# A three-branch hybrid layer: decays carried in place in the third branch's scan, and another split of the attention's products

## The chip, the cores and the metric

The kernel runs on one core of a Trainium2 chip, as one launch. The number reported is the device time of one execution in microseconds; the figure for the kernel before is the median of three such runs, 2732.86 us (2730.51 to 2734.73). A separate execution was taken by the hardware profiler; it took 2729.9 us, and its span, from the first instruction to the last, is 2728.1 us.

The core's engines work side by side, each through its own instructions in order: TensorE (PE, with its weight loads shown as PEld), VectorE (DVE), ScalarE (ACT), GpSimd (POOL), and SyncE (SP), which here issues the DMAs. They meet only at semaphores.

## The reference, cut to what matters

Sixteen meta tokens go ahead of 2048 tokens of width 1024. After a normalization, one wide projection feeds three mixers of four heads each (head size 128): stick-breaking attention, a gated delta rule, and HGRN2. Their outputs are gated, projected back and summed. The change lies in the first and the third.

The attention's weight of a key is its own sigmoid times the product of the "not taken" sigmoids of all later keys:

```python
log_keep = jnp.where(mask, jax.nn.log_sigmoid(-z), 0.0)
log_passed = lax.cumsum(log_keep, axis=3, reverse=True) - log_keep
attn = jnp.where(mask, jnp.exp(jax.nn.log_sigmoid(z) + log_passed), 0.0)
```

The third branch is a linear recurrence whose state decays per channel; inside a chunk every pair of tokens i >= j needs the product of the decays between them:

```python
a = jnp.einsum('bhid,bhjd,bhijd->bhij', q_c, k_c, dec)
o = o_inter + jnp.einsum('bhij,bhje->bhie', a, v_c)
state = state * jnp.exp(g_end)[:, :, 0, :, None] + jnp.einsum('bhcd,bhce->bhde', k_c * jnp.exp(g_end - g_c), v_c)
```

## The kernel before, in words

**Quarters and dense work.** The 2048 tokens are worked in four quarters of 512 (j = 0 to 3). A generator, `dense_work`, makes all projections of a quarter, the branch products and the output projection: groups of 8 x 3 matmuls of 512 columns. Every fp32 value is split into a rounded high part and a low remainder, and a product is three passes, high by high, high by low, low by high (`mm3`, L176 to L178). A second set of generators makes the sequential parts: `sb_scan` (attention, one head at a time), `gdn_mats` and `gdn_scan` (second branch), `hg_scan` (third branch, two heads at a time, so two passes a quarter and eight in all). `weave` interleaves a scan with dense work by planned microseconds: a scan's `yield 5.0` lets about so much dense work be written between two of its steps. The tile framework then orders the instructions of each engine by its own timeline model, so what stands in the program may move a little.

**The attention's scan.** For each block of keys and each of four 128-query tiles i, `weights` makes the scores z on TensorE, two sigmoids on ScalarE (L533, L534), copies the carry of the block before into the end of `pc` (L538, GpSimd), a running product over the keys on VectorE (L539), and multiplies the sigmoid by it (L545, `at`). That product is on VectorE for tiles 0 and 2 and on GpSimd for tiles 1 and 3. `values` then transposes the four tiles (L567), rounds the high part on ScalarE (L578) and forms the low part on VectorE (L127), and adds to the output `av` by three passes: `mm3` with lh, ll the values' high and low part and ath, atl the weights' high and low part. The order of passes is lh by ath, lh by atl, ll by ath.

**The third branch's scan.** `hg_scan` finds the within-chunk matrix by seven levels, s = 1, 2, 4 ... 64. At level s the chunk is cut into pairs of blocks of s tokens; the rows of the right block against the columns of the left one are a plain product, once each query carries the decays from its block's start and each key those to its block's end. The kernel before keeps two running decay tiles per head, `pf` (from the block's start, in place of the forget gate) and `sf` (to the block's end). At each level, for each head, VectorE writes a fresh tile `kql`: right halves q x pf (L1151), left halves k x sf (L1155; at s = 1 a copy on GpSimd, L1153). TensorE multiplies it with itself in small tiles into `z` (L1160), VectorE or ScalarE picks the wanted parts (L1208, L1195, L1202), and VectorE brings `sf` and `pf` to the next block size (L1223, L1224; at s = 1 a copy and a fill on GpSimd, L1220, L1221). After the last level q x pf and k x sf are formed over 512 tokens (L1231, L1233), the latter is transposed to tokens, and a scan over four sub-blocks of 128 updates the state (L1244 to L1249). Each kql is a tile of its own in a pool of 21 buffers (tag S), so VectorE may make the next levels' while TensorE has not reached them.

## Time and profile before

| | |
|---|---|
| median of three runs | 2732.86 us |
| profiled execution | 2729.9 us, span 2728.1 us |
| PE busy | 2690.0 us, 99% of the span |
| PEld, DVE, ACT, POOL busy | 2243.4, 1432.5, 961.0, 717.7 us |
| granted TensorE clock, mean | 0.999 |

In the rows of groups, "acc<-xh,w ... x2096 | 796.8, 380" gives how many records there are, their busy time in us, and the mean of one in ns; what stands after the next bar is the engine's idle time ahead of them and what ended it. Matmuls overlap in the pipeline, so their durations add to more than the time that passes. A matmul of fp32 operands that is no transpose has two records. The table by windows gives, for stretches of the span, the busy time of each engine.

### The profile page before, as it was taken

The numbers are of one execution on the slowest core, as the hardware profiler recorded it, in microseconds if no ns is written. First come the engines' busy times: TensorE is split into PE (matmuls) and PEld (weight loads), VectorE is DVE, ScalarE is ACT, GpSimd is POOL, SyncE is SP. The second block draws the span as 40 slices with busy tenths as digits, with TensorE's granted clock in tenths as the row PEclk, the third lists the DMA queues.
The fourth block names the chain that finished last, engine by engine and source line by source line (L and its number), as shares of the span: only waits on it lengthen the run. The fifth ranks groups of instructions, "written<-read, shape, count | busy, mean of one in ns | idle before, by whom it ended". The sixth has DMA issues, their size and how long they took to land.

```text
span 2728.1 us, 46691 instructions
## 1 busy us (share of the span) xinstructions
PE 2690.0 (99%) x17984; PEld 2243.4 (82%) x17984; DVE 1432.5 (53%) x2870; ACT 961.0 (35%) x2199; POOL 717.7 (26%) x989
## 2 busy tenths in 40 slices
PE   7999999999999999999999999999999999999999
PEld 6998888888888888888888888888888887787887
DVE  5476647645357734443255765554325568556422
ACT  5564343343346212212144641321214456313120
POOL 4555213433133401112122332111212223302111
PEclk9999999999999999999999999999999999999999
DMA  7667756679554654557755456355774454554556
GB/s 263 221 234 251 256 178 221 231 268 320 195 180 146 205 177 130 157 158 241 231 190 171 156 168 205 106 158 155 248 221 140 163 168 143 164 161 122 160 163 213
DMA packets 200834, 521.08 MB, mean 191 GB/s; under 512 B 42848, under 2 KB 44832, under 8 KB 200612
## 3 DMA queue, kind: packets, MB, share of 16 engines
q1 hardware_dynamic: 200324, 518.03, 59.0%
q8 instruction: 142, 2.33, 0.3%
q14 instruction: 80, 0.66, 0.1%
q10 hardware_dynamic: 288, 0.07, 0.0%
HBM read 397.57 MB, written 120.44 MB: 190 GB/s over the span
## 4 chain that ended last, share of the span: by engine, by line
PE 92%; DVE 5%; DMA 1%; ACT 1%; issue 1%; POOL 0%; SPq 0%; DVEq 0%; ACTq 0%; POOLq 0%
PE acc L176 20%; PE acc L177 20%; PE acc L178 20%; PE av L176 5%; PE av L177 5%; PE av L178 5%; PE tr L567 2%; PE t L389 2%; PE z L1160 1%; PE z L176 1%; PE z L177 1%; PE z L178 1%; PE z L864 1%; PE tr L389 1%; PE tr L1245 1%
## 5 line engine op out<-in xcount | busy, mean ns | idle before, releaser
L176 PE MATMUL acc<-xh,w 128*128 128x512 f32 (+2 forms) x2096 | 796.8, 380 | 5.6 <-DVE y L1293 1.7
L177 PE MATMUL acc<-xl,w 128*128 128x512 f32 (+2 forms) x2096 | 790.0, 377 | 0.3 <-DVE xl L269 0.2
L178 PE MATMUL acc<-xh,w 128*128 128x512 f32 (+2 forms) x2096 | 786.7, 375 | 0.0
L176 PEld LDWEIGHTS acc<-xh,w 128*128 128x128 f32 x2096 | 396.1, 189 | 75.2 <-DVE y L1293 2.2
L178 PEld LDWEIGHTS acc<-xh,w 128*128 128x128 f32 x2096 | 396.4, 189 | 66.2 <-issue 0.2
L177 PEld LDWEIGHTS acc<-xl,w 128*128 128x128 f32 x2096 | 395.9, 189 | 65.2 <-DVE xl L269 1.3
L539 DVE TENSOR_TENSOR_SCAN S<-S,zero 128x128 f32<-128x128 f32 (+4 forms) x216 | 196.7, 913 | 113.8 <-ACT S L533 107.1
L127 POOL TENSOR_TENSOR w<-wraw,w 128x512 fp32r<-128x512 f32 x106 | 147.3, 1392 | 239.9 <-ACT w L156 222.4
L545 POOL TENSOR_TENSOR S<-S,S 128x256 f32<-128x256 f32 (+2 forms) x108 | 96.5, 894 | 367.1 <-DVE S L539 190.7
L176 PE MATMUL av<-xh,w 128*128 128x512 f32 (+2 forms) x440 | 172.7, 392 | 0.0
L177 PE MATMUL av<-xl,w 128*128 128x512 f32 (+2 forms) x440 | 171.9, 391 | 0.0
L178 PE MATMUL av<-xh,w 128*128 128x512 f32 (+2 forms) x440 | 171.3, 389 | 0.0
L156 ACT CAST w<-wraw 128x512 fp32r<-128x512 f32 x182 | 112.6, 619 | 142.4 <-PE acc L178 70.9
L533 ACT ACTIVATE S<-z,rq 128x128 f32<-128x128 f32 (+4 forms) x216 | 117.3, 543 | 117.7 <-PE z L178 90.2
L745 DVE SCALAR_TENSOR_TENSOR D<-D,cw,D 128x512 f32<-128x512 f32 (+1 forms) x144 | 119.0, 833 | 21.3 <-ACT D L743 19.8
L127 DVE TENSOR_TENSOR S<-tr,S 128x512 fp32r<-128x512 f32 (+4 forms) x176 | 105.9, 607 | 42.7 <-ACT S L572 24.0
L1297 POOL TENSOR_TENSOR y<-y,g 128x512 f32<-128x512 f32 x32 | 48.2, 1507 | 288.9 <-DVE g L1295 288.9
L176 PE MATMUL acc<-ob,w 128*128 128x512 f32 x296 | 118.0, 399 | 1.4 <-ACT ob L410 1.4
L177 PE MATMUL acc<-ob,w 128*128 128x512 f32 x296 | 117.7, 398 | 0.0
L178 PE MATMUL acc<-ob,w 128*128 128x512 f32 x296 | 117.6, 397 | 0.0
L534 ACT ACTIVATE S<-z,rq 128x128 f32<-128x128 f32 (+4 forms) x216 | 117.0, 542 | 0.0
L133 POOL TENSOR_SCALAR nu<-nv 128x8 f32<-128x8 f32 (+3 forms) x39 | 14.8, 379 | 334.2 <-DVE nv L1065 193.6
(407 smaller groups left out, 4978.2 us busy)
## 6 DMA issues: line engine op xcount, KB each, us to landing
w<-wk SPq DMA_DIRECT2D x555, 512.0 KB, 3.7
wk<-w SPq DMA_DIRECT2D x184, 512.0 KB, 3.5
wraw<-in_w_in_dram SPq DMA_DIRECT2D x142, 256.0 KB, 4.0
D<-in_xq_dram SPq DMA_DIRECT2D x56, 256.0 KB, 4.6
S<-rows SPq DMA_DIRECT2D x48, 256.0 KB, 5.2
S<-dv SPq DMA_DIRECT2D x48, 256.0 KB, 4.8
out_dram<-D SPq DMA_DIRECT2D x32, 256.0 KB, 4.6
S<-dk SPq DMA_DIRECT2D x24, 264.0 KB, 3.9
```

The lines of the kernel that those rows point to most:

```text
L127: (eng or nc.gpsimd).tensor_sub(out_, a, hi.bitcast(F32))
L156: nc.scalar.copy(hi, raw)
L176: nc.tensor.matmul(dst, lh, rh, start=first, stop=False)
L177: nc.tensor.matmul(dst, lh, rl, start=False, stop=False)
L178: nc.tensor.matmul(dst, ll, rh, start=False, stop=last)
L389: nc.tensor.transpose(pt[:, n * P : (n + 1) * P], src[:, META + n * P : META + (n + 1) * P], ident)
L533: nc.scalar.activation(pc[:, :n], z[:, :n], AF.Sigmoid, scale=rq[:, NT + i : NT + i + 1])
L534: nc.scalar.activation(at[:, :n], z[:, :n], AF.Sigmoid, scale=rq[:, i : i + 1])
L539: nc.vector.tensor_tensor_scan(pc[:, 0:n][:, ::-1], pc[:, 0:n][:, ::-1], zero1.broadcast_to([P, n]), 1.0 if carry[i] is None else pc[:, n ...
L545: eng.tensor_mul(at[:, :n], at[:, :n], pc[:, 1 : n + 1])
L567: nc.tensor.transpose(tr[:kw, i * P : (i + 1) * P], ats[i][:, a - lo : a - lo + kw], ident)
L745: nc.vector.scalar_tensor_tensor(dst[:, c0:], raw[:, c0 + i : c0 + i + n], cw[:, ci, i : i + 1], dst[:, c0:], ALU.mult, ALU.add)
```

## The change

It does four things.

In `hg_scan`, `kql` and `sf` are gone. A tile `qf` per head holds the queries, in its right halves multiplied by the decays at once (VectorE, L1158) and in its left halves too (GpSimd, L1159); the keys stay in `kk`. TensorE multiplies `kk` by `qf` directly. After each level the left halves of `kk` are multiplied in place by the total decay of the right block (L1224), the right halves of `qf` in place by the total of the left block (L1225), and a small tile `tt` takes the product of the two totals for the next level (L1226, 256 elements at s = 1, then 128, 64, ... 4). After the last level `qf` and `kk` are what L1231 and L1233 made before, so these are gone; the state's decay comes from the last totals.

In `sb_scan`, L545 puts tiles 0 and 2 on GpSimd and tiles 1 and 3 on VectorE. The three passes of `product` are written out, lh by ath, ll by ath, lh by atl: the pass with the weights' low part is the third, not the second.

```diff
--- before.py
+++ after.py
@@ -541,7 +541,7 @@
                     1.0 if carry[i] is None else pc[:, n : n + 1], ALU.mult, ALU.add,
                 )
                 carry[i] = pc
-                eng = nc.gpsimd if i % 2 else nc.vector
+                eng = nc.vector if i % 2 else nc.gpsimd
                 eng.tensor_mul(at[:, :n], at[:, :n], pc[:, 1 : n + 1])
                 ats[i] = at
                 yield 0.4 + n * 0.0045
@@ -556,7 +556,10 @@
                     nc.tensor.matmul(av, vm, ath[:96], start=not started[0], stop=last)
                 else:
                     lh, ll = svh[:, kt * P : (kt + 1) * P], svl[:, kt * P : (kt + 1) * P]
-                    mm3(av[:, cs_], lh, ll, ath[:, cs_], atl[:, cs_], not started[0], last)
+
+                    nc.tensor.matmul(av[:, cs_], lh, ath[:, cs_], start=not started[0], stop=False)
+                    nc.tensor.matmul(av[:, cs_], ll, ath[:, cs_], start=False, stop=False)
+                    nc.tensor.matmul(av[:, cs_], lh, atl[:, cs_], start=False, stop=last)
                 started[0] = True
 
             left = None
@@ -1136,7 +1139,11 @@
 
         pf, kk, qq, vt, gate = zip(*(st.pop(h) for h in hs))
         two = range(2)
-        sf = [slot("S") for _ in two]
+
+
+        qf = [slot("S") for _ in two]
+        tt = [slot("S") for _ in two]
+        off, prev = 0, None
         s = 1
         lv = 0
         while s < P:
@@ -1145,14 +1152,11 @@
                 return r_[:, :, 0], r_[:, :, 1]
 
             nb = TQ // (2 * s)
-            kql = [slot("S") for _ in two]
-            for i in two:
-                kl_, kr_ = v4(kql[i])
-                nc.vector.tensor_mul(kr_, v4(qq[i])[1], v4(pf[i])[1])
-                if s == 1:
-                    nc.gpsimd.tensor_copy(kl_, v4(kk[i])[0])
-                else:
-                    nc.vector.tensor_mul(kl_, v4(kk[i])[0], v4(sf[i])[0])
+            if s == 1:
+                for i in two:
+                    ql_, qr_ = v4(qf[i])
+                    nc.vector.tensor_mul(qr_, v4(qq[i])[1], v4(pf[i])[1])
+                    nc.gpsimd.tensor_mul(ql_, v4(qq[i])[0], v4(pf[i])[0])
             z = p_z()
             last = None
 
@@ -1170,7 +1174,7 @@
                             c, o = META + n * P, 64 * (n % 2)
                             m = 2 * i + n // 2
                             last = mm(
-                                z[o : o + 64, m * 64 : m * 64 + 64], kql[i][:, c : c + 64], kql[i][:, c + 64 : c + P]
+                                z[o : o + 64, m * 64 : m * 64 + 64], kk[i][:, c : c + 64], qf[i][:, c + 64 : c + P]
                             )
                     elif s == 32:
                         for n in range(NT):
@@ -1178,12 +1182,12 @@
                                 c, o = META + n * P + b, b + 32 * (n % 2)
                                 m = 2 * i + n // 2
                                 last = mm(
-                                    z[o : o + 32, m * 32 : m * 32 + 32], kql[i][:, c : c + 32],
-                                    kql[i][:, c + 32 : c + 64],
+                                    z[o : o + 32, m * 32 : m * 32 + 32], kk[i][:, c : c + 32],
+                                    qf[i][:, c + 32 : c + 64],
                                 )
                     else:
 
-                        pairs = [(kql[i], kql[i])] + ([(kk[i], qq[i])] if s == 1 else [])
+                        pairs = [(kk[i], qf[i])] + ([(kk[i], qq[i])] if s == 1 else [])
                         for q, (lh, rh) in enumerate(pairs):
                             for n in range(NT):
                                 for b in range(0, P, 32):
@@ -1214,25 +1218,21 @@
                         sl = slice(32 * b, 32 * b + 32)
                         nc.scalar.copy(AT[sl, :, :, sl], AD[sl].rearrange("p (i n) c -> p i n c", i=2))
             for i in two:
-                pl_, pr_ = v4(pf[i])
-                fl_, fr_ = v4(sf[i])
-                if s == 1:
-                    nc.gpsimd.tensor_copy(fl_, pr_)
-                    nc.gpsimd.memset(fr_, 1.0)
-                else:
-                    nc.vector.tensor_mul(fl_, fl_, pr_[:, :, s - 1 : s].broadcast_to([P, nb, s]))
-                nc.vector.tensor_mul(pr_, pr_, pl_[:, :, s - 1 : s].broadcast_to([P, nb, s]))
+                tl_, tr_ = v4(pf[i]) if s == 1 else (prev[i][:, 0::2, None], prev[i][:, 1::2, None])
+                kl_ = v4(kk[i])[0]
+                qr_ = v4(qf[i])[1]
+                nc.vector.tensor_mul(kl_, kl_, tr_.broadcast_to([P, nb, s]))
+                nc.vector.tensor_mul(qr_, qr_, tl_.broadcast_to([P, nb, s]))
+                nc.vector.tensor_mul(tt[i][:, off : off + nb, None], tl_, tr_)
+            prev = [t[:, off : off + nb] for t in tt]
+            off += nb
             s *= 2
             lv += 1
             yield 5.0
-        qe, ke, ket, os_ = [], [], [], []
+        ket, os_ = [], []
         for i in two:
-            qe.append(slot("S"))
-            nc.vector.tensor_mul(qe[i][:, META:], qq[i][:, META:], pf[i][:, META:])
-            ke.append(slot("S"))
-            nc.vector.tensor_mul(ke[i][:, META:], kk[i][:, META:], sf[i][:, META:])
             ket.append(slot("S", (P, NT, P)))
-            nc.scalar.copy(ket[i].rearrange("p a b -> p (a b)"), to_tokens(ke[i], p_tr()))
+            nc.scalar.copy(ket[i].rearrange("p a b -> p (a b)"), to_tokens(kk[i], p_tr()))
             os_.append(slot("S"))
         ssq = slot("ssq", (P, 2 * NT), F32, 3)
         yield 4.0
@@ -1241,12 +1241,11 @@
             for i, h in enumerate(hs):
                 p1 = p_tr()
                 dst = p1[:, :P]
-                nc.tensor.matmul(dst, qe[i][:, cs], Sh[h], start=True, stop=False)
+                nc.tensor.matmul(dst, qf[i][:, cs], Sh[h], start=True, stop=False)
                 nc.tensor.matmul(dst, AT[:, i, n], vt[i][:, n], start=False, stop=True)
                 pS = p1[:, P : 2 * P]
                 nc.tensor.matmul(pS, ket[i][:, n], vt[i][:, n], start=True, stop=True)
-                e = META + (n + 1) * P - 1
-                nc.vector.scalar_tensor_tensor(Sh[h], Sh[h], pf[i][:, e : e + 1], pS, ALU.mult, ALU.add)
+                nc.vector.scalar_tensor_tensor(Sh[h], Sh[h], prev[i][:, n : n + 1], pS, ALU.mult, ALU.add)
                 nc.vector.tensor_copy(os_[i][:, cs], dst)
                 junk = slot("junk", (P, P), F32, 2)
                 m = NT * i + n
```

Three places show what this does to the instructions' order.

TensorE, first of the two passes of the last quarter, around the levels s = 16 and 32. In the rows before, S_25806 and S_25805 are the kql of heads 1 and 0 at s = 16, S_25875 and S_25874 those at s = 32.

```order
L177 MATMUL av_25867<-xl_20773,w_4957_25865 128x512
L178 MATMUL av_25867<-xh_20772,w_4957_25865 128x512
L1160 MATMUL z_25811<-S_25806 32x32 x16
L1160 MATMUL z_25811<-S_25805 32x32 x16
L1160 MATMUL z_25880<-S_25875 32x32 x8
L1160 MATMUL z_25880<-S_25874 32x32 x8
L176 MATMUL av_25867<-xh_20810,w_4957_25865 128x512
```

In the rows of the change, S_25312 and D_24457 are qf and kk of head 0, S_25313 and D_25176 those of head 1.

```order
L176 MATMUL acc_25794<-xh_20428,w_4871_25790 128x512
L177 MATMUL acc_25794<-xl_20429,w_4871_25790 128x512
L1164 MATMUL z_25601<-S_25312,D_24457 32x32 x16
L1164 MATMUL z_25666<-S_25313,D_25176 32x32 x8
L178 MATMUL acc_25794<-xh_20428,w_4871_25790 128x512
L176 MATMUL acc_25794<-xh_20466,w_4871_25790 128x512
```

Before, level 32 followed level 16 with no dense matmul between; now, for one and the same head, dense matmuls stand between any two levels from s = 2 on: 14 to 23 of 512 columns in this pass. In the second passes it is 15 between s = 1 and 2, then 20 or 21, against 12 to 15 before.

VectorE, second pass of the last quarter, some levels. Before, D_25861 and D_26269 are pf, S_26456 and S_26457 sf, S_26559 to S_26687 kql of one head or the other.

```order
L1151 TENSOR_TENSOR S_26559<-D_26304,D_26269 128x128x2
L1155 TENSOR_TENSOR S_26619<-D_25862,S_26456 128x64x4
L1223 TENSOR_TENSOR S_26457<-S_26457,D_26269 128x128x2
L1151 TENSOR_TENSOR S_26619<-D_25948,D_25861 128x64x4
L1223 TENSOR_TENSOR S_26456<-S_26456,D_25861 128x64x4
L1224 TENSOR_TENSOR D_26269<-D_26269 128x128x2
L1155 TENSOR_TENSOR S_26620<-D_26270,S_26457 128x64x4
L1224 TENSOR_TENSOR D_25861<-D_25861 128x64x4
L1151 TENSOR_TENSOR S_26620<-D_26304,D_26269 128x64x4
L1155 TENSOR_TENSOR S_26687<-D_25862,S_26456 128x32x8
```

Now, with D_26046 and S_26233 the kk and qf of head 1, D_25654 and S_26232 those of head 0:

```order
L1224 TENSOR_TENSOR D_26046<-D_26046,S_26235 128x128x2
L1225 TENSOR_TENSOR S_26233<-S_26233,S_26235 128x128x2
L1212 COPY_PREDICATED AD<-lvl,z_26334 128x256
L1224 TENSOR_TENSOR D_25654<-D_25654,S_26234 128x128x2
L1225 TENSOR_TENSOR S_26232<-S_26232,S_26234 128x128x2
L1224 TENSOR_TENSOR D_26046<-D_26046,S_26235 128x64x4
L1225 TENSOR_TENSOR S_26233<-S_26233,S_26235 128x64x4
L1212 COPY_PREDICATED AD<-lvl,z_26391 128x256
```

Before, VectorE's rows went from level to level without a row that reads TensorE's result; now each level's pick (L1212, which reads z) and the in-place products, which may write only after TensorE has read, stand in one line, level after level.

The end of the attention's last head in the last quarter. VectorE before (S_23435, S_23451 are `pc` of tiles 2 and 3, S_23436 `at` of tile 2; tile 3's product stood on GpSimd):

```order
L539 SCALAR_TENSOR_TENSOR S_23406<-S_23406,zero_383 128x272
L127 TENSOR_TENSOR S_23419<-tr_23413,S_23418 128x512
L539 SCALAR_TENSOR_TENSOR S_23435<-S_23435,zero_383 128x272
L539 SCALAR_TENSOR_TENSOR S_23451<-S_23451,zero_383 128x272
L545 TENSOR_TENSOR S_23436<-S_23436,S_23435 128x272
```

Now (S_23243, S_23259 are `pc` of tiles 2 and 3, S_23260 `at` of tile 3; tile 2's product stands on GpSimd):

```order
L545 TENSOR_TENSOR S_23215<-S_23215,S_23214 128x272
L127 TENSOR_TENSOR S_23227<-tr_23221,S_23226 128x512
L539 SCALAR_TENSOR_TENSOR S_23243<-S_23243,zero_383 128x272
L539 SCALAR_TENSOR_TENSOR S_23259<-S_23259,zero_383 128x272
L545 TENSOR_TENSOR S_23260<-S_23260,S_23259 128x272
```

The last product of the block now follows its own scan on the same engine, and GpSimd's last one belongs to the tile before, whose scan ends one scan earlier.

## The prediction

> **What bounds the kernel now.** I read the page's engine shares first, then the table by windows, then what TensorE waited for.
>
> ```profile
> span 2728.1 us, 46691 instructions
> PE 2690.0 (99%) x17984; PEld 2243.4 (82%) x17984; DVE 1432.5 (53%) x2870; ACT 961.0 (35%) x2199; POOL 717.7 (26%) x989
> ```
>
> TensorE is busy in 99% of the span. The change leaves every matmul in place: same number, shapes and types, only other operands. So the time can move in two ways alone: TensorE waits less or more, or a matmul takes longer in another neighbourhood. Where does it wait?
>
> ```profile
> 30.00:360.00 330.00, 323.48 (x2266) 288.40 (x2265) 191.96 (x359) 162.26 (x365) 158.34 (x198) 0.99 0.73 246
> 365.00:1010.00 645.00, 644.82 (x4344) 537.81 (x4344) 365.06 (x723) 247.34 (x569) 196.59 (x246) 1.00 0.64 212
> 1010.00:1690.00 680.00, 680.00 (x4206) 561.71 (x4205) 340.72 (x676) 223.30 (x502) 144.71 (x224) 1.00 0.57 180
> 1690.00:2350.00 660.00, 649.98 (x4251) 533.18 (x4250) 350.88 (x662) 241.16 (x534) 145.44 (x220) 1.00 0.52 165
> 1765.00:1791.00 26.00, 24.39 (x511) 18.94 (x505) 25.20 (x58) 3.34 (x11) 7.39 (x5) 1.00 0.45 133
> 2484.00:2510.00 26.00, 24.47 (x500) 18.93 (x487) 25.17 (x59) 3.45 (x10) 7.19 (x5) 1.00 0.46 135
> 2574.00:2600.00 26.00, 26.00 (x519) 20.02 (x517) 10.06 (x16) 3.84 (x10) 4.36 (x3) 1.00 0.48 160
> 2333.00:2350.00 17.00, 10.97 (x62) 8.17 (x61) 10.79 (x15) 5.20 (x13) 7.09 (x12) 1.00 0.46 121
> ```
>
> After the length of a window come the busy times of PE, PEld, DVE, ACT and POOL. Between 365 and 1690 us TensorE misses 0.18 us of 1325; there is nothing to gain there, whatever VectorE does. It misses 10.0 us between 1690 and 2350. Two places stand out. The first passes of the third branch in the third and fourth quarter (1765 and 2484) lose 1.6 and 1.5 us, with VectorE busy 25.2 of 26 us. The end of the last quarter's attention (2333 to 2350) loses 6.0 us: no dense work is left beside it. A second pass (2574) loses nothing, with VectorE at 10.1 of 26.
>
> From 360 us to the end, TensorE waited for:
>
> ```profile
> PE z L1160 <- DVE S L1151: 2.3, 2, 1.4
> PE av L556 <- ACT S L574: 2.0, 1, 2.0
> PE acc L176 <- DVE y L1293: 1.7, 1, 1.7
> PE acc L176 <- ACT ob L410: 1.4, 1, 1.4
> PE acc L176 <- ACT D L1091: 1.1, 2, 0.6
> PE acc L176 <- DMA w<-wk: 0.9, 2, 0.6
> PE tr L567 <- DVE S L545: 0.8, 1, 0.8
> PE t L389 <- ACT D L767: 0.7, 1, 0.7
> PE av L177 <- DVE S L127: 0.7, 2, 0.5
> ```
>
> The columns are us in all, times, and the longest; two rows of 0.2 are left out. All of it is 11.6 us, 0.4% of the time: the bound of what the change could bring after 360 us. Before 360 us another 6.5 us are missed, in the first quarter.
>
> **The change part by part.** All durations are from the profiled execution, 2729.9 us, so the sum is made against that; the median shown is 3.0 us above it, and the difference is carried over to the median.
>
> *The third branch: VectorE's load.*
>
> ```profile
> L1151 DVE TENSOR_TENSOR S<-D,D 128x256 f32<-128x256 f32 x112 | 53.7, 482 | 0.1
> L1155 DVE TENSOR_TENSOR S<-D,S 128x256 f32<-128x256 f32 x96 | 43.9, 457 | 0.0
> L1223 DVE TENSOR_TENSOR S<-S,D 128x256 f32<-128x256 f32 x96 | 47.9, 498 | 0.0
> L1224 DVE TENSOR_TENSOR D<-D 128x256 f32<-128x256 f32 x112 | 54.6, 488 | 0.6 <-POOL S L1220 0.6
> L1231 DVE TENSOR_TENSOR S<-D,D 128x512 f32<-128x512 f32 x16 | 14.2, 886 | 0.0
> L1233 DVE TENSOR_TENSOR S<-D,S 128x512 f32<-128x512 f32 x16 | 14.2, 887 | 0.0
> L1208 DVE COPY_PREDICATED AD<-lvl,z 128x256 f32<-128x256 uint8 x48 | 21.1, 440 | 36.2 <-PE z L1160 36.0
> 2320.47 0.15 DVE L789 TENSOR_TENSOR aq<-nr 128x4 f32<-128x4 f32 x1
> ```
>
> The first six groups go: 53.7 + 43.9 + 47.9 + 54.6 + 14.2 + 14.2 = 228.5 us in eight passes, 28.6 us a pass. In their place a pass has 2 + 14 + 14 products of 256 elements, 30 x 0.48 = 14.4 us, and 14 products of totals. Those run from 256 elements (0.48) down to 4 (0.15, the last row); half are of 32 or fewer, so I take 0.25 each, 3.5 us. VectorE falls from 28.6 to 17.9 us a pass, 86 us in all. TensorE feels this only in the two windows where VectorE was full; after it, VectorE would have some 25.2 - 9 = 16 of 26 us there, between the full window and the second pass that lost nothing. So the 2.3 us of waits of L1160 for L1151 go: **-2.3 us** (bounds 0 and the two windows' whole loss, 3.1). The rest of the 86 us lies under a TensorE that was busy anyway and brings nothing.
>
> *The third branch: the new chain.* In place, a level's products must wait until TensorE has read the level, and TensorE's next level waits for them. Before, the kql tiles let VectorE run ahead. What does a link cost?
>
> ```profile
> 2498.65 0.67 DVE L1295 TENSOR_TENSOR g<-g,acc 128x512 f32<-128x512 f32 x1
> 2503.70 0.41 DVE L1151 TENSOR_TENSOR S<-D,D 128x256 f32<-128x256 f32 x1
> 2504.26 0.46 PE L1160 MATMUL z<-S 128*32 128x32 f32 x32 [0.89 <-DVE S L1151]
> 2325.56 0.39 PE L176 MATMUL acc<-ob,w 128*128 128x512 f32 x1
> 2325.79 0.39 PE L177 MATMUL acc<-ob,w 128*128 128x512 f32 x1
> 2499.41 1.41 POOL L1297 TENSOR_TENSOR y<-y,g 128x512 f32<-128x512 f32 x1 [1.29 <-DVE g L1295]
> 2499.59 1.51 DVE L1151 TENSOR_TENSOR S<-D,D 128x256 f32<-128x256 f32 x1
> 2483.65 2.96 POOL L127 TENSOR_TENSOR ob<-S,ob 128x512 fp32r<-128x512 f32 x2
> 2483.96 1.50 DVE L1223 TENSOR_TENSOR S<-S,D 128x256 f32<-128x256 f32 x1
> L545 POOL TENSOR_TENSOR S<-S,S 128x256 f32<-128x256 f32 x40 | 32.9, 824 | 165.5 <-ACT S L533 60.8 <-DVE S L539 59.6 <-ACT D L426 13.8
> ```
>
> An undisturbed product takes 0.41 us, and TensorE starts 0.15 us after it (2503.70 + 0.41 to 2504.26). From the end of a level: one hand-over, the pick (0.44), four products (1.64), one hand-over, 2.4 us in all. What covers it: dense matmuls follow each other by 0.23 us (2325.56 to 2325.79), so the 20 between two levels of a second pass are 4.6 us, the 15 after s = 1 are 3.5, and the 14 to 23 per head in the two first passes 3.2 to 5.3. The link fits, and with one product of a gate in VectorE's queue (L1295, 0.67) it is 3.1 and still does.
>
> It is less sure beside GpSimd. L1151 took 1.51 us instead of 0.41 beside L1297, and L1223 1.50 beside L127: up to 1.1 us more. The Trainium skill, "SBUF — State Buffer", section "Who interferes with whom", has a rule for this: a VectorE instruction with two inputs in SBUF and a GpSimd instruction that reads SBUF exclude each other, and the later one blocks until the other is done. The two pairs of rows agree. By that rule a blocked link would be 3.5 us, 0.3 past the shortest cover of 3.2; with that in both first passes the sum below would be -1.5 instead of -2.1.
>
> One place has little cover. In the first passes of the third and fourth quarter, head 1 comes from s = 1 to s = 2 with two dense matmuls (0.46 us) and its neighbour's small ones (0.46 for 32 records, in the row at 2504.26) between, 0.9 us, against two products and two hand-overs, 1.1 us, or 2.2 with one block; and it is there (2483.65) that GpSimd worked on L127. The excess is 0.2 to 1.3 us; I put 0.5 on each, nearer the unblocked end, because GpSimd now reaches L127 without the fills and copies ahead of it: **+1.0 us** (bounds 0 and 2.6). On GpSimd, two products (L1159) come for four copies and two fills in a pass. In the attention's rows such a product takes 0.82 us; GpSimd is idle 74% of the span, which hides it.
>
> *The end of a pass.* The levels stand further apart, so the state's scan of the last pass comes some 4 us of dense work later, and its outputs have about 1 us less until the branch product. The list has no wait of a branch product there: nothing, and at most the 1 us by which the room shrinks.
>
> *The attention's passes.* Each of the three passes loads its own weights (17984 loads for 17984 matmul records in the page); the swap saves and costs none. The low part has 0.23 us more before it is wanted. Two waits stood there, 0.7 us together: each shrinks by 0.23, **-0.5 us** (bounds 0 and -0.7).
>
> *The attention's products.* The same 54 pairs, tiles exchanged.
>
> ```profile
> 2335.35 0.42 DVE L545 TENSOR_TENSOR S<-S,S 128x272 f32<-128x272 f32 x1
> 2335.61 0.69 POOL L545 TENSOR_TENSOR S<-S,S 128x272 f32<-128x272 f32 x1 [1.55 <-DVE S L539]
> 2335.82 1.03 PE L567 MATMUL tr<-ident,S 128*32 128x128 f32 x6 [0.77 <-DVE S L545]
> ```
>
> Tile 3's product ended at 2336.30 on GpSimd; on VectorE it would follow its scan and end near 2335.85, while GpSimd does tile 2's beside that scan, which may stretch it by some tenths. Only here is nothing dense beside it: **-0.3 us** (bounds +0.5 and -0.5). Elsewhere the transposes wait behind dense work.
>
> **The sum:** -2.3 + 1.0 - 0.5 - 0.3 = -2.1 us: 2727.8 us for a profiled execution, 2730.8 for the median (-0.08%). By the bounds alone, -3.1 - 0.7 - 0.5 = -4.3 to 2.6 + 1.0 + 0.5 = +4.1.
>
> **The rivals.** *One wait for another.* The first passes keep their loss: VectorE no longer lags, but head 1 waits at s = 2, and at each later level something small. For it: at present VectorE may run ahead by seven levels, and all that goes. Against: covers of 3 to 5 us. Then the 2.3 are not gained, and the attention's 0.8 is all: 2732.1.
>
> *All small waits go.* VectorE is 86 us lighter, so evacuations, casts behind it and weight buffers come sooner. Of the waits listed, those outside the attention's end are 2.3 + 1.1 + 0.9 + 0.7 + 0.7 = 5.7 us; with 0.8 of the end, 6.5: 2726.4. For it: the waits for L1091, L767 and w fall in busy stretches. Against: they have ScalarE and DMA at their end, not VectorE.
>
> *Slower: the chain shows.* In each of the 48 gaps between levels the products are blocked by GpSimd once or twice. With two blocks and a gate's product a link is 2.4 + 0.7 + 2.2 = 5.3 us, over the 4.6 by 0.7 and over the first gap's 3.5 by 1.8. In a quarter of all gaps that is 10 x 0.7 + 2 x 1.8 = 10.6 us; with the 3.1 gained of -2.3, -0.5 and -0.3, 2740.4. It decides from a link of 4.6 us on. For it: the stretched rows. Against: GpSimd has 4 to 7 us of work in such a window of 26, so most links meet none.
>
> *It doesn't do what it says:* should GpSimd's copies of the carry now queue behind tile 2's product, the last scan would start later by 0.7 us, in one place. That is inside the range.
>
> **How the numbers follow.** The forecast (2730.8) 0.42, one wait for another 0.20, all small waits 0.26, slower 0.12. A change under 0.2%, 5.5 us, can't be told from none in a measurement of this kernel. The first two cases are within it, the third past it, the fourth beyond it on the other side: faster 0.26, within 0.62, slower 0.12. The likeliest case's own range is 2728.5 to 2737.0 by the bounds; with the faster case's price below it, I take 2724.5 to 2737.
>
> **What would show it.** Right: VectorE near 1345 us in the page; the two windows' PE within 0.5 us of full; L1164's waits for L1224 and L1225 under 1.5 us in all; the attention's end still some 6 us short. Wrong: a list of waits in which z at L1164 stands ahead of all others with many entries (the chain), or PE's gaps unchanged in sum while the median falls by over 5 us, which would mean that matmuls themselves got shorter, against all that is said here.

## The result, and the profile after

The change makes the kernel slower: 2750.6 us, median of six runs (2742.9 to 2755.0), against 2730.16 us for the kernel before beside it; the ratio is 1.0069, 95% interval 1.0058 to 1.0080. Forecast were 2730.8 us and, with 0.12, a slower kernel; the time lies 13.6 us above the range. The profiled execution of the changed kernel took 2755.0 us, 25.1 more than that of the kernel before; it is the slowest of the six. The six follow the granted clock of the whole run: 2742.9 and 2744.2 us at 1.000 and 0.999, 2750.2 to 2755.0 at 0.996 and 0.997.

The page of the changed kernel, its span and its engines:

```profile
span 2753.1 us, 46635 instructions
PE 2702.8 (98%) x17984; PEld 2250.9 (82%) x17984; DVE 1385.8 (50%) x2774; ACT 958.4 (35%) x2199; POOL 699.1 (25%) x957
```

The matmuls are as many as before. VectorE has 46.7 us less to do, and it bought nothing. What TensorE waited for from 360 us on, the first rows and three on the attention (us in all, times, longest):

```profile
PE z L1164 <- DVE D L1224: 5.2, 2, 2.6
PE acc L176 <- ACT D L1278: 2.7, 2, 1.5
PE tr L570 <- POOL S L545: 2.5, 2, 1.6
PE acc L176 <- DVE D L1294: 2.1, 1, 2.1
...
PE av L560 <- ACT S L581: 1.5, 2, 0.9
...
PE av L560 <- DMA w<-wk: 1.3, 1, 1.3
PE av L562 <- DVE S L127: 1.2, 3, 0.5
```

None of the first four rows stood in the list of before; L1160's wait for L1151 (2.3) is gone. The whole list adds up to 23.9 us; before it was 12.0 (11.6 in the prediction, which left out two rows of 0.2). Where they lie, and the clock, by windows:

```profile
365.00:1010.00 645.00, 642.70 (x4333) 536.15 (x4333) 354.58 (x698) 246.99 (x572) 185.57 (x238) 1.00 0.64 211
1768.00:1794.00 26.00, 23.34 (x428) 17.84 (x428) 16.77 (x41) 3.01 (x5) 8.29 (x6) 0.93 0.40 120
2497.00:2523.00 26.00, 23.34 (x369) 18.13 (x368) 18.75 (x49) 3.04 (x6) 8.28 (x6) 0.87 0.36 108
2351.00:2368.00 17.00, 10.18 (x57) 7.15 (x55) 10.73 (x17) 7.21 (x17) 5.22 (x11) 1.00 0.38 91
1777.80:1781.20 3.40, 3.40 (x10) 2.61 (x9) 1.09 (x4) 0.00 (x0) 0.00 (x0) 0.50 0.00 0
2508.30:2515.10 6.80, 6.27 (x45) 5.00 (x46) 2.70 (x12) 0.00 (x0) 0.00 (x0) 0.50 0.00 0
```

The second quarter's stretch (365 to 1010), which missed 0.2 us before, misses 2.3. The two first passes of the third branch (1768 and 2497) now lose 2.7 us each, with VectorE at 17 to 19 of 26 us: the load fell as forecast, and the loss grew. And at each of them, beginning within 1.1 us of the wait's end, stands a stretch of 3.4 or 6.8 us with a granted clock of 0.50. Such stretches come to 23.9 us in this profile (seven of 3.41 us, the one at 2508 being two), and to 3.4 us in that of before, the idle end left out of both.

Two kinds of loss are to be explained, then: the waits, and the half clock. They account for most of the difference in a simple way. From the span I take the waits (from 30 us on, as the profile lists them) and half of the time at half clock:

| profile | span | waits | at half clock | rest |
|---|---|---|---|---|
| before | 2728.1 | 18.4 | 3.4 | 2708.0 |
| changed | 2753.1 | 29.9 | 23.9 | 2711.3 |
| scan alone (below) | 2743.6 | 25.6 | 17.1 | 2709.5 |
| scan mended (below) | 2725.6 | 13.8 | 10.2 | 2706.7 |
| whole change mended (below) | 2718.2 | 10.3 | 6.8 | 2704.5 |

The rest is the same within 0.3% in all eighteen profiles of this study (2704.5 to 2712.3); that is a range of 7.8 us, so the split says little of smaller differences. Of the 25.0 us that the span grew, 11.5 are waits and 10.3 half clock; 3.3 are left over.

### The profile page after: what moved, and what is told of

It is laid out like the page before. It is cut to its first block, busy times and chain, and to the rows that moved or that the text cites. A ratio compares the mean times of both kernels' runs of the same rounds, so it can differ in the third digit from the quotient of the medians.

```text
span 2753.1 us, 46635 instructions
## 1 busy us (share of the span) xinstructions
PE 2702.8 (98%) x17984; PEld 2250.9 (82%) x17984; DVE 1385.8 (50%) x2774; ACT 958.4 (35%) x2199; POOL 699.1 (25%) x957
## 4 chain that ended last, share of the span: by engine, by line
PE 93%; DVE 4%; ACT 1%; issue 1%; DMA 1%; POOL 0%; SPq 0%; DVEq 0%; ACTq 0%; POOLq 0%
PE acc L176 20%; PE acc L177 20%; PE acc L178 20%; PE av L177 4%; PE av L176 4%; PE av L178 4%; PE tr L570 2%; PE t L389 2%; PE z L1164 1%; PE av L562 1%; PE z L176 1%; PE z L177 1%; PE z L178 1%; PE av L561 1%; PE av L560 1%; PE z L867 1%
## 5 line engine op out<-in xcount | busy, mean ns | idle before, releaser
L176 PE MATMUL acc<-xh,w 128*128 128x512 f32 (+2 forms) x2096 | 796.7, 380 | 10.2 <-ACT D L1278 2.7
L539 DVE TENSOR_TENSOR_SCAN S<-S,zero 128x128 f32<-128x128 f32 (+4 forms) x216 | 203.4, 949 | 116.9 <-ACT S L533 86.3
L127 POOL TENSOR_TENSOR w<-wraw,w 128x512 fp32r<-128x512 f32 x106 | 141.2, 1334 | 262.6 <-ACT w L156 232.4
L545 POOL TENSOR_TENSOR S<-S,S 128x128 f32<-128x128 f32 (+4 forms) x108 | 92.6, 858 | 392.8 <-DVE S L539 260.8
L127 DVE TENSOR_TENSOR S<-tr,S 128x512 fp32r<-128x512 f32 (+4 forms) x176 | 106.4, 608 | 47.4 <-ACT S L581 22.9
L1296 POOL TENSOR_TENSOR y<-y,g 128x512 f32<-128x512 f32 x32 | 43.8, 1367 | 293.7 <-DVE g L1294 290.1
L570 PE MATMUL tr<-ident,S 128*128 128x128 f32 (+1 forms) x608 | 103.0, 272 | 2.5 <-POOL S L545 2.5
```

The costliest lines, as they stand in the source:

```text
L127: (eng or nc.gpsimd).tensor_sub(out_, a, hi.bitcast(F32))
L176: nc.tensor.matmul(dst, lh, rh, start=first, stop=False)
L539: nc.vector.tensor_tensor_scan(pc[:, 0:n][:, ::-1], pc[:, 0:n][:, ::-1], zero1.broadcast_to([P, n]), 1.0 if carry[i] is None else pc[:, n ...
L545: eng.tensor_mul(at[:, :n], at[:, :n], pc[:, 1 : n + 1])
L570: nc.tensor.transpose(tr[:kw, i * P : (i + 1) * P], ats[i][:, a - lo : a - lo + kw], ident)
```

## The experiments

**The three parts apart.** The scan alone (the attention put back), the exchange of engines alone, and the order of the passes alone:

```diff
# scan alone, against the changed kernel
-                eng = nc.vector if i % 2 else nc.gpsimd
+                eng = nc.gpsimd if i % 2 else nc.vector
...
+                    mm3(av[:, cs_], lh, ll, ath[:, cs_], atl[:, cs_], not started[0], last)
# engines alone, against the kernel before
-                eng = nc.gpsimd if i % 2 else nc.vector
+                eng = nc.vector if i % 2 else nc.gpsimd
# passes alone, against the kernel before
-                    mm3(av[:, cs_], lh, ll, ath[:, cs_], atl[:, cs_], not started[0], last)
+                    nc.tensor.matmul(av[:, cs_], lh, ath[:, cs_], start=not started[0], stop=False)
+                    nc.tensor.matmul(av[:, cs_], ll, ath[:, cs_], start=False, stop=False)
+                    nc.tensor.matmul(av[:, cs_], lh, atl[:, cs_], start=False, stop=last)
```

> The third branch's scan in place alone; the attention as in the kernel before. Theory: the loss is the scan's. TensorE's waits for L1224 (5.2 us in the changed kernel, 2.6 each in the first passes of the third and fourth quarter) and its waits where a scan's end meets the next quarter's norm statistics (2.1 and 2.7 us) stand here too, and behind them stretches of 3.4 us in which the clock is granted at half: 2741 to 2748 us, 0.4 to 0.65% over the kernel before. Rival (the loss is the exchange of the products between VectorE and GpSimd): 2729 to 2733 us.

> The exchange of the attention's products between VectorE and GpSimd alone (L545). Theory: the transposes of the last quarter wait for GpSimd's tiles, some 4 us in all, 2733 to 2736 us. Rival (the exchange is the loss): 2745 us or more. Rival (it is hidden, as predicted): within 1 us of the kernel before.

> The order of the three passes alone (the pass with the weights' low part last). All theories: 0 to -0.7 us against the kernel before, not to be told from none; two waits of L177 for the low part (0.7 us) go or shrink.

Measured: the scan 2743.02 us, ratio 1.0047 (1.0034 to 1.0061); the engines 2735.67, 1.0024 (1.0013 to 1.0034); the passes 2730.65, 1.0008 (0.9999 to 1.0017), against 2729.49. In us +13.5, +6.2 and +1.2, together 20.9; the whole change cost 20.4. So the parts add up, the scan carries two thirds, and the passes are not to be told from nothing. The runs below stand beside different runs of the kernel before (medians from 2728.6 to 2731.4 us), so differences between them are taken from the ratios where that matters; each ratio has an interval of about 3 us to either side.

**The scan's first gap.** What held head 1 at the step from s = 1 to s = 2? The changed kernel's timeline at the third quarter's first pass (start, us, engine, line):

```profile
1768.96 5.60 POOL L127 TENSOR_TENSOR ob<-S,ob 128x512 fp32r<-128x512 f32 x4 [5.41 <-ACT ob L410]
1769.94 2.05 DVE L1158 TENSOR_TENSOR S<-D,D 128x256 f32<-128x256 f32 x2
1771.91 2.94 DVE L1226 TENSOR_TENSOR S<-D 128x256 f32<-128x256 f32 x2
1774.77 1.06 DVE L1226 TENSOR_TENSOR S<-S 128x128 f32<-128x128 f32 x7
1775.75 0.42 DVE L1225 TENSOR_TENSOR S<-S,D 128x256 f32<-128x256 f32 x1
1776.08 0.24 DVE L1226 TENSOR_TENSOR S<-S 128x16 f32<-128x16 f32 x2
1776.25 0.42 DVE L1224 TENSOR_TENSOR D<-D,D 128x256 f32<-128x256 f32 x1
...
1773.74 0.40 PE L178 MATMUL av<-ob,w 128*128 128x512 f32 x1
1776.72 0.46 PE L1164 MATMUL z<-S,D 128*32 128x32 f32 x32 [2.58 <-DVE D L1224]
1778.41 0.63 PE L177 MATMUL av<-ob,w 128*128 128x512 f32 x1
```

The framework has put the chain of totals (L1226), which needs nothing from TensorE, ahead of the first product. Two of these instructions take 2.94 us beside GpSimd's 5.60 us of L127, where two such take 0.75 undisturbed (in the timeline of the order after the first level, below); nine smaller ones and L1225 follow, and L1224 starts 4.3 us after the first total, 1.7 after L127's end (1774.56). Without the totals the product could have started at that end and TensorE 0.47 us behind it, as here: by these rows 1.7 of the 2.58 us are for the totals and 0.9 for GpSimd's block. That is an estimate. Then TensorE's matmuls stand 0.43 us apart (1778.41 to 1778.84 in the same view) instead of 0.23: the half clock.

To take the totals out of the way, VectorE's order is kept at every level: both heads' products first, then the totals.

```diff
-            for i in two:
-                tl_, tr_ = v4(pf[i]) if s == 1 else (prev[i][:, 0::2, None], prev[i][:, 1::2, None])
+            tot = [v4(pf[i]) if s == 1 else (prev[i][:, 0::2, None], prev[i][:, 1::2, None]) for i in two]
+            pin = tc.keep_in_program_order
+            for i in (1, 0):
...
-                nc.vector.tensor_mul(kl_, kl_, tr_.broadcast_to([P, nb, s]))
-                nc.vector.tensor_mul(qr_, qr_, tl_.broadcast_to([P, nb, s]))
-                nc.vector.tensor_mul(tt[i][:, off : off + nb, None], tl_, tr_)
+                pin(nc.vector.tensor_mul(kl_, kl_, tot[i][1].broadcast_to([P, nb, s])))
+                pin(nc.vector.tensor_mul(qr_, qr_, tot[i][0].broadcast_to([P, nb, s])))
+            for i in (1, 0):
+                pin(nc.vector.tensor_mul(tt[i][:, off : off + nb, None], *tot[i]))
```

> The changed kernel, with VectorE's instructions of a level kept in this order: the two products of head 1, the two of head 0, then the totals for the next level (in the changed kernel the totals of all levels stand ahead of the first product). Theory: the two waits of 2.6 us are the chain of totals ahead of the product, blocked by GpSimd at L127; they shrink to below 1 us each, and the half-clock stretches at 1778 and 2508 us (3.4 and 6.8 us, 5 us of time) go with them: 5 to 9 us below the changed kernel, 2741 to 2746 us. Rival (the product itself is late for TensorE, whatever stands ahead of it): the waits stay at 2 us or more and the time within 3 us of the changed kernel's 2750.6.

Measured: 2753.7 us, 1.0090 (1.0077 to 1.0104). Both were half right. The waits of z for the products are gone from the list altogether, and no half clock stands near 1778 or 2508 us. But half clock stands elsewhere, 23.9 us of it as in the changed kernel, and others took their place; the first two of its list that are new or larger, from 360 us on (here L1296 is the changed kernel's L1294):

```profile
PE acc L176 <- DVE D L1296: 4.5, 3, 2.3
PE acc L176 <- ACT ob L410: 4.3, 4, 1.4
```

They lie at the ends of the quarters: with the totals in the chain at every level, the scan ended later still (around 600 us, GpSimd begins on the last pass's outputs at 604.26 in place of 602.82). So the order is kept after the first level only, and the attention is put back, to see the scan by itself.

```diff
-            pin = tc.keep_in_program_order
+            pin = tc.keep_in_program_order if s == 1 else (lambda x: x)
```

> The third branch's scan in place alone (the attention as before), with VectorE's order kept after the first level only: both heads' products, then the first totals; the totals of the other levels stay free. Theory: the two waits of 2.6 us for the product go, and with them the half-clock stretch at 1777 us; the waits at the quarters' ends stay or grow, since the scan ends no earlier: 2736 to 2741 us, against 2743.0 for the scan alone. Rival (any order of these products only moves the loss to the quarters' ends): 2742 to 2746 us.

Measured: 2734.83 us, 1.0016 (1.0006 to 1.0025), against 1.0047 for the scan alone: 8.5 us less, and a little more than was expected. At the same place in its timeline (L1222 and L1223 are the products, L1225 the totals, L1161 the small matmuls):

```profile
1764.30 5.42 POOL L127 TENSOR_TENSOR ob<-S,ob 128x512 fp32r<-128x512 f32 x4 [5.40 <-ACT ob L410]
1769.63 0.41 DVE L1222 TENSOR_TENSOR D<-D,D 128x256 f32<-128x256 f32 x1
1769.96 0.42 DVE L1223 TENSOR_TENSOR S<-S,D 128x256 f32<-128x256 f32 x1
1770.97 0.75 DVE L1225 TENSOR_TENSOR S<-D 128x256 f32<-128x256 f32 x2
...
1775.14 0.76 PE L1161 MATMUL z<-S,D 128*32 128x32 f32 x64
```

L127 still takes 5.42 us in one go, but the products start as it ends, with no total ahead of them, and run in 0.41. TensorE's order has moved too, however: between the small matmuls of s = 1 and those of s = 2 (1775.14) it now has 27 dense ones, where the changed kernel had two for head 1. So the run shows that the order of the two queues was the loss. How much of it lay in VectorE's totals and how much in TensorE's short cover it doesn't tell; for that there is only the estimate above. Its list of waits has now one large row, at three quarters' ends:

```profile
PE acc L176 <- DVE D L1293: 4.6, 3, 1.6
```

**The quarters' ends.** The kernel before, and the changed one, around 600 us, where the last pass's outputs (L127 on GpSimd) meet the next quarter's norm statistics (L356 on VectorE). Before:

```profile
596.61 2.54 POOL L127 TENSOR_TENSOR ob<-S,ob 128x512 fp32r<-128x512 f32 x2
600.72 2.28 DVE L356 TENSOR_TENSOR D<-D,D 128x512 f32<-128x512 f32 x3
```

After:

```profile
602.82 1.30 POOL L127 TENSOR_TENSOR ob<-S,ob 128x512 fp32r<-128x512 f32 x1 [3.71 <-ACT ob L410]
603.30 4.65 DVE L356 TENSOR_TENSOR D<-D,D 128x512 f32<-128x512 f32 x4 [0.36 <-ACT D L352]
604.38 1.43 POOL L127 TENSOR_TENSOR ob<-S,ob 128x512 fp32r<-128x512 f32 x1 [0.27 <-DMA wraw<-in_w_br_dram]
610.60 0.80 PE L176 MATMUL acc<-xh,w 128*128 128x512 f32 x1 [2.12 <-DVE D L1294]
```

Before, GpSimd was done 1.6 us before the statistics began, and three of these took 2.28 us; after, the two fall together, four take 4.65, and what stands behind them on VectorE and ScalarE (L1294, L1278) is late. If the scan's later end is the cause, an earlier begin must undo it. One unit of dense work ahead of the second pass is put behind it, in the changed kernel, in the kernel of the last experiment, and in the kernel before as a control.

```diff
-        adv(6 if j >= AHEAD else 5)
+        adv(5 if j >= AHEAD else 4)
         for h, o_ in enumerate(weave(hg_scan(j, (2, 3), hst), 2 * HG_US, 6)):
             obs[2, 2 + h] = o_
-        adv(8)
+        adv(9)
```

> The changed kernel with the second pass of the third branch begun one unit of dense work earlier in each quarter (and one more unit after it). Theory: the waits of TensorE at the quarters' ends for L1294 and L1278 (2.1, 1.5 and 1.2 us near 610, 1261 and 1945 us) come from the scan's later end, whose outputs' low parts on GpSimd then fall beside the next quarter's norm statistics on VectorE; with the earlier begin each falls below 0.5 us and the half-clock stretch at 610 us goes: 4 to 8 us below the changed kernel, 2743 to 2747 us. Rival (the statistics are late by themselves, whatever the scan does): the three waits stay and the time is within 3 us of 2750.6.

> The same, and the second pass of each quarter one unit of dense work earlier. Theory: both kinds of wait are gone, and what the prediction expected of the scan is left: 2727 to 2731 us, not above the kernel before. Rival (something else in the scan costs: matmuls that run longer, or waits not yet seen): 2734 us or more.

> The kernel before with the second pass of each quarter one unit of dense work earlier, as a control. No theory here says that the shift is worth anything by itself: within 2 us of the kernel before. If it gains 3 us or more, the earlier begin is a gain of its own and says nothing of the changed scan.

Measured: the changed kernel with it 2742.32 us, 1.0039 (1.0027 to 1.0052), 8.2 us less by the ratios than without; the mended scan 2728.05, 0.9985 (0.9977 to 0.9994); the control 2730.27, 0.9996 (0.9987 to 1.0005). The waits for L1294 and L1278 are gone from both lists of the changed scan; the control never had them. In the changed kernel GpSimd is now done 4.1 us before the statistics begin:

```profile
590.18 2.55 POOL L127 TENSOR_TENSOR ob<-S,ob 128x512 fp32r<-128x512 f32 x2 [0.53 <-ACT ob L410]
596.85 1.49 DVE L356 TENSOR_TENSOR D<-D,D 128x512 f32<-128x512 f32 x2 [6.80 <-ACT D L352]
```

What TensorE still waits for in the mended scan, first row:

```profile
PE av L556 <- ACT S L574: 2.0, 1, 2.0
```

Here the prediction's own step stands alone at last: the carry in place, against the control, is worth 2728.05 - 2730.27 = -2.2 us, and neither L1151's nor L1224's wait is in the list. The sum had put it at -2.3 + 1.0. The two intervals overlap, so that the mended scan is no slower is shown, and that it is faster than the control is not.

**The attention's engines.** My theory was that GpSimd's product comes too late for the transposes. Three other assignments of L545 tell: all four tiles on VectorE (in the kernel before and in the mended scan), tiles 0 and 1 exchanged alone, and tiles 2 and 3 alone.

```diff
-                eng = nc.gpsimd if i % 2 else nc.vector
+                eng = nc.vector                                   # all on VectorE
+                eng = nc.gpsimd if i in (0, 3) else nc.vector     # tiles 0 and 1 exchanged
+                eng = nc.gpsimd if i in (1, 2) else nc.vector     # tiles 2 and 3 exchanged
```

> The kernel before with the attention's products of all four tiles on VectorE (L545). Theory: what the exchange cost (6.2 us) is a product on GpSimd that the transposes wait for; with none on GpSimd these waits are gone, and VectorE, 53% busy, hides 54 products more of the four-tile blocks: 2728 to 2732 us, within 2 us of the kernel before. Rival (VectorE's queue is what makes it late; the two more products stand ahead of the casts and scans that TensorE waits for): 2734 us or more.

> The scan in place with the order after the first level kept and the second pass one unit earlier (2728.05 us), with the four products on VectorE as well. Theory: VectorE has 48 us less to do in this kernel, the transposes wait for nothing on GpSimd: 2725 to 2729 us. Rival (VectorE's queue): 2731 us or more.

> The kernel before with tiles 0 and 1 exchanged alone (0 and 3 on GpSimd, 1 and 2 on VectorE). Theory: the transposes run through the tiles in turn and wait for the third's product on GpSimd (the wait of 1.1 us for a product of 384 elements); tile 0's product is long done by then: within 1.5 us of the kernel before. Rival (any tile on another engine shifts the casts behind it): 2733 us or more.

> The kernel before with tiles 2 and 3 exchanged alone (1 and 2 on GpSimd, 0 and 3 on VectorE). Theory: most of the exchange's loss of 6.2 us is here: 2733 to 2737 us, with TensorE's transposes waiting for GpSimd's L545 for 1 us or more. Rival: within 1.5 us of the kernel before.

Measured: all on VectorE 2736.12, 1.0030 (1.0019 to 1.0040); on the mended scan 2732.82, 1.0013 (1.0003 to 1.0022); tiles 0 and 1 2735.96, 1.0026 (1.0015 to 1.0036); tiles 2 and 3 2733.18, 1.0021 (1.0012 to 1.0030). The theory falls: any assignment but the old one costs 4.6 to 7.5 us, with no product on GpSimd too. What have they in common? TensorE around the last head's last scores (L530 ends them) in the last quarter, before:

```profile
2275.56 0.23 PE L530 MATMUL z<-neg_b,ident_b 128*128 128x128 bf16 x1
2275.59 0.47 PE L177 MATMUL acc<-xl,w 128*128 128x512 f32 x1
...
2281.49 0.39 PE L178 MATMUL acc<-xh,w 128*128 128x512 f32 x1
2281.72 0.39 PE L176 MATMUL z<-S,D 128*128 128x512 f32 x1
2281.95 0.49 PE L567 MATMUL tr<-ident,S 128*128 128x128 f32 x3
```

With the engines exchanged alone:

```profile
2276.70 0.23 PE L530 MATMUL z<-neg_b,ident_b 128*128 128x128 bf16 x1
2276.74 0.48 PE L177 MATMUL acc<-xl,w 128*128 128x512 f32 x1
...
2277.74 0.39 PE L178 MATMUL acc<-xh,w 128*128 128x512 f32 x1
...
2278.20 0.38 PE L567 MATMUL tr<-ident,S 128*128 128x128 f32 x2
2279.91 0.33 PE L567 MATMUL tr<-ident,S 128*128 128x128 f32 x1 [1.09 <-POOL S L545]
```

And with tiles 0 and 1 alone, where the third tile's product is VectorE's as before:

```profile
2278.63 1.27 DVE L545 TENSOR_TENSOR S<-S,S 128x384 f32<-128x384 f32 x1 [0.20 <-ACT D L801]
2279.96 0.33 PE L567 MATMUL tr<-ident,S 128*128 128x128 f32 x1 [1.80 <-DVE S L545]
```

Before, 26 dense matmuls (6.0 us) lie between the last score and the transposes; with the engines exchanged 5, with tiles 0 and 1 exchanged 4, in the changed kernel 3; with tiles 2 and 3 exchanged or all on VectorE it is 5 too. The other 20 or so have been written ahead of the last two tiles' scores, where nobody needs them. The framework orders TensorE by its own model of the other engines, and another assignment gave another order. To put that to the test, the scores of a diagonal block in the last quarter are written without dense work between them, and the block's share after the fourth, in the kernel with the engines exchanged and, as a control, in the kernel before.

```diff
-                yield 0.4 + n * 0.0045
+                yield 0.4 + n * 0.0045 if (s < j or j < 3) else (7.6 if i == NT - 1 else 0.0)
```

> The exchange of the products alone, but in the last quarter the scores of a diagonal block's four tiles are written without dense work between them, and the block's share of it after the fourth. In TensorE's order 24 dense matmuls then stand again between the last head's last scores and their transposes (26 in the kernel before, 5 with the exchange alone). Theory: it is this order that costs; the waits of the transposes for L545 near 2280 us go: 2728 to 2732 us. Rival (the engines themselves, or the casts behind them): 2734 us or more.

> The kernel before with the same writing of the last quarter's scores, as a control. TensorE's order at the last head's last scores is nearly as before (26 dense matmuls behind them): within 2 us of the kernel before.

Measured: 2726.33 us, 0.9988 (0.9979 to 0.9997), against 1.0024 with the exchange alone: 9.8 us less by the ratios with the same engines, and with 24 dense matmuls in that place again. The control: 2729.62, 0.9999 (0.9990 to 1.0008). So it was the order, not the engines. By which wait the order costs is less clear: from 360 us on the list falls from 15.7 to 8.8 us, and only 1.4 of that is the transposes' waits for L545; the rest is mainly spread over six other rows.

**The whole change, mended.** All parts of the change with the two orders of the scan mended, and then with the scores too.

> The whole change with the two orders of the scan mended, the attention as changed. Theory: the attention's cost of some 6 us is left above the 2728.05 us of the mended scan alone: 2732 to 2737 us, with a wait of the transposes for L545 of over 1 us in the last quarter.

> The whole change with three orders mended: VectorE's after the first level, the second pass one unit earlier, and the scores of the last quarter's diagonal blocks together. Theory: the three causes are all there is; 2727 to 2732 us. Rival (a further cost in the changed kernel): 2735 us or more.

Measured: 2733.53 us, 1.0017 (1.0009 to 1.0026), and 2721.3, 0.9972 (0.9962 to 0.9983). The last beats both kernels, by 8 and 29 us, and by more than was expected of it; from 360 us on its list adds up to 5.9 us, against 12.0 in the kernel before, and which edit took each of the small waits away is not settled. The earlier begin and the new order of the scores gave the kernel before nothing one at a time; both together were not tried in it, so how much of the 8 us is the change's own is not shown. Its page, and the first of its waits:

```profile
span 2718.2 us, 46604 instructions
PE 2688.5 (99%) x17984; PEld 2244.6 (83%) x17984; DVE 1357.1 (50%) x2774; ACT 960.9 (35%) x2199; POOL 703.1 (26%) x957
...
PE av L556 <- ACT S L577: 2.0, 1, 2.0
PE acc L176 <- ACT ob L410: 1.4, 1, 1.4
```

## Why the prediction was wrong

**What bounds the kernel**: right. TensorE was busy in 98% of the span after, and all but 3.3 of the 25 us lost in the profile are waiting or clock. That a lighter VectorE brings nothing by itself held.

**VectorE's load**: right in kind, too large in size. From groups of the changed kernel:

```profile
L1224 DVE TENSOR_TENSOR D<-D,S 128x256 f32<-128x256 f32 x96 | 49.3, 513 | 67.3 <-PE z L1164 67.3
L1226 DVE TENSOR_TENSOR S<-D 128x256 f32<-128x256 f32 x16 | 15.4, 1004 | 0.0
```

All groups of the new scan add up to 160 us, not the 143 of eight passes at 17.9: the 240 products took 0.53 on the mean, not 0.48, and the 112 totals 0.30, not 0.25, those over 256 elements 1.0. By rows the scan is 69 us lighter, not 86. VectorE's busy time fell by 46.7 only. Rows of VectorE overlap (1769.63 and 1769.96 above, of 0.41 and 0.42 us), so groups add up to more than busy time, 1549 against 1432.5 us before, and the prediction took the one from the other. In the mended scan the busy time falls by 76 (to 1356.5). The wait of L1160 for L1151, **-2.3**, went as forecast.

**The new chain**, costed at **+1.0**: the place was right to the step (head 1 from s = 1 to s = 2 in the first passes of quarters 3 and 4, and no other link in the list), and the reason it would be small was wrong. The step that failed reads "because GpSimd now reaches L127 without the fills and copies ahead of it". Without them L127 ran in one go of 5.6 us, and it was VectorE that had something new ahead of the product: the whole chain of totals. The excess was 2.6 each, not 0.5, and past the 1.3 of the upper bound, by the estimate above because of the totals; at both places half clock stood beside it. I had counted the totals as load (3.5 us a pass) and not asked where they stand in VectorE's queue. That they had been moved ahead can be read from the written order: in the rows shown with the change no total stands between two levels.

**The end of a pass**, costed at **nothing**: a wrong step about as dear as the chain. I had the shift (some 4 us) and looked for a wait of the branch product, and no row gave the 1 us by which I let its room shrink; the work that the outputs ran into was the next quarter's norm statistics. Three waits came there, 4.8 us in all, and with the earlier begin that takes them away the kernel is 8.2 us faster.

**The passes**, **-0.5**: not seen; +1.2 us with an interval that holds zero. Three waits for the low part, 1.2 us, are there after.

**The attention's products**, **-0.3**: wrong, +6.2. I looked at the end of the last quarter's attention, where the loss stayed nearly as it was (6.8 of 17 us in the window from 2351, 6.0 before). "Elsewhere the transposes wait behind dense work" is the sentence that failed: it took TensorE's order for given, and the change moved 20 dense matmuls away from just there.

**The rivals.** "The chain shows" had the sign and a neighbouring place, but not the mechanism: it had many links a little late, while one link was very late and the rest never. Its 2740.4 was 10 us short, for want of the quarters' ends, the attention and the clock. "One wait for another" holds for the one step of the chain.

**The half clock** was in no term and no rival. About 10 us of the profiled difference hang on it, in the slowest of the six runs; at a clock of 1.000 the changed kernel still took 2742.9 us, past the range.

## What to carry to other kernels

Before a change is costed, compare the written order of every engine at the places where the bounding engine has little cover, and price what now stands ahead of the instruction it waits for; a planner that reorders by its own model may cost more than the edit brings, and may be told the order. Where a stage ends later, look at what the next stage does then on the engines that it shares, not at its own consumer alone. And when a change with a sound mechanism measures slow, look for the order before the mechanism is given up: here the same arithmetic ranged from 2721 to 2754 us.

## What the runs showed of the hardware

**Half clock beside short waits of TensorE.** In the profile of the changed kernel, one or two stretches of 3.41 us with a granted clock of 0.50 stood at each of the three longest waits from 360 us on, 2.1 to 2.6 us each (610, 1777 and 2508 us), and began between 0.6 us before the wait's end and 1.1 us behind it; matmuls stood 0.43 us apart in them instead of 0.23, some 1.7 us lost in each. It does not follow every such wait: the changed kernel with the earlier begin has the same two waits of 2.6 us for L1224 (1765 and 2495 us), with a granted clock of 1.00 around both. None stood at the 1.5 at 1261 us, or the 2.0 and 1.4 at 2359 in the changed kernel, and some stood elsewhere in one run and not in another (50.7 us in the changed kernel, none there in the kernel before). So the half clock makes the time of the changed kernel scatter, 2742.9 to 2755.0 us, where the kernel before has 2727.6 to 2734.7; but the four runs with VectorE's order kept at every level, all at a clock of 0.996, lie within 1.3 us. The Trainium skill, "TensorE: Matmul & The Clock Gate", Part 1, tells of a clock gate at 4/8 or 8/8 and of a free-running window of 3413 ns; under "HAM oscillation" it reckons half of the throttled time as the penalty. The stretches of 3.41 us at 0.50 and the table of the result agree. Its advice there, no idle gaps over about 3.4 us, would not have warned of these: half clock stood at a wait of 2.1 us. What decides it, the place of the wait in the window or the work around it, was not tried; that the waits bring it is argued from where it stands, not shown.

**VectorE beside GpSimd.** Two products of 256 elements took 2.94 us beside L127 and 0.75 us without it, four sums of 512 elements 4.65 us beside it where three took 2.28 without. So the engines meet at more than the semaphores named at the start: these rows stretch with GpSimd's work beside them. The prediction knew this stretch and priced one block of 1.1 us; what it lacked was how much of VectorE's queue would stand there.
